# HGRN projections as seven of eight block products, head squares summed by ScalarE, and a VectorE copy of the last norm's factors

## The chip, the cores and the metric

The program runs on one core of a Trainium2 chip. The core has a matrix engine (TensorE, PE in the profile; its weight loads are listed as PEld), a vector engine (VectorE, DVE), a scalar engine (ScalarE, ACT), a general engine (GpSimd, POOL), and an engine that here only issues transfers (SyncE, SP). Each runs its own list of instructions in order and waits on semaphores for the others. The metric is the device time of one execution in microseconds (us); less is better.

## The reference

The reference is a trunk of two layers on one sequence of 1024 tokens with 1024 features, all in fp32. Each layer is a token mixer and a gated convolutional FFN, each behind an RMS norm whose scale, shift and gate come from a conditioning vector. Layer 0 mixes with a gMLP spatial gate, layer 1 with HGRN2, and a last RMS norm closes the trunk. The change lies in the HGRN2 mixer and in the last norm:

```python
def hgrn2_mixer(h, w_in, lb, gn_g, w_out):
    q, fz, i, g = jnp.split(h @ w_in, 4, axis=-1)
    f = lb + (1.0 - lb) * jax.nn.sigmoid(fz)
    k, q = 1.0 - f, jax.nn.silu(q)
    o = hgrn2_chunked_scan(heads(q), heads(k), heads(i), heads(jnp.log(f)))
    o = o * lax.rsqrt(jnp.mean(o * o, axis=-1, keepdims=True) + EPS)
    return (o.reshape(bsz, t, HG_HEADS * HG_VAL) * gn_g * jax.nn.silu(g)) @ w_out
...
x = x + g1 * y
...
return rms_norm(x, final_g)
```

There are 8 heads of 128 features. The scan gives `out[t] = q[t] . state[t]` with `state[t] = f[t] * state[t-1] + k[t] v[t]`, where v is i.

## The kernel before

**Number format.** Every large matrix product is done on pairs: an operand is split into a rounded part `hi` (made by ScalarE) and a rest `lo` (the source minus `hi`, made by VectorE or GpSimd), and `mm3` (line 272) issues three matmuls for each 128x128 block: hi·hi, hi·lo, lo·hi. `p_split` (lines 470 and 473) makes such a pair; its argument "V" or "G" says who subtracts.

**Order.** The kernel doesn't issue as it goes. Every step is entered in a list (`pl.op`) with its engine, an expected duration, what it reads and writes, and a place `pr`. A list scheduler runs over the steps once at the end with these durations, and the order it finds is the order of the instructions of each engine (and of the transfers, all of which SyncE issues). It treats GpSimd and those VectorE steps that are marked `port` as excluding each other.

**Stages.** In order: gMLP input products, spatial gate, output product; FFN of layer 0; HGRN2; its output product; FFN of layer 1; the last norm. Activations lie with features on partitions; the tokens form two halves, LO and HI, of 512 each. The residual `xT` (128 partitions x 8 feature blocks x 1024 tokens) stays in SBUF.

**Strassen-Winograd in the other stages.** The gMLP input products and the FFN (class `Pairs`) take two 128-row weight blocks at a time and cut weights and activations into 2x2 blocks: seven block products (`PRODUCTS`) in place of eight. Some products need sums of activation blocks (T1 to T4, built once by `combos`), others sums of weight blocks (built for each pair by `pair`: four VectorE sums, four pairs split by VectorE and three by GpSimd). `pair` also moves the products out of PSUM: `snap` copies by ScalarE, `add` adds by VectorE (line 701). The first pairs of a stage go the plain way with eight block products, while the sums are built. The output products (`block_out`, seven products named P1 to P7 in their order) use the same scheme.

**HGRN2 before.** Sixteen units, two for each head (LO and HI). For a unit, `project` computes f, q and g with `h_proj`, all eight block products: 3 x 24 matmuls of 512 columns. The values i come from `iproj` for two heads at a time with the tokens on partitions, as the scan needs them: 24 matmuls of 256 columns for each of 8 token blocks. `scan` then runs seven levels (line 1487 the matmuls, 1493 and 1497 the doubling steps of VectorE and ScalarE, 1470, 1519 and 1531 the score blocks), the state update (1549 to 1567), the outputs (1576, 1578), the head's norm (1580 squares by ScalarE, 1582 their sums by VectorE, a chain of ten small VectorE instructions, 1590 the scaling by VectorE), a transpose (1598) and the gain and gate (1600). Projections of the next unit stand between the scan's steps in PE's order. Units use banks 0 to 2 for projections, 3 and 4 for levels, 5 to 7 for the rest.

**Into the stage.** FFN 0 ends with the last block product; `f0_last` evacuates it into `xT` (412), sums squares, forms the norm's factors (333, the chain, 338, 343), and `ln_p` normalises each feature block: 448 by VectorE, then either hi by ScalarE (457) and lo by VectorE (458), or for every other block of HI two ScalarE steps and lo by GpSimd (462 to 464).

**The end.** `f1_last` works on the last 512 tokens in two parts of 256. Part 1's factors are copied from PSUM to SBUF by ScalarE (347), since GpSimd uses them from there; GpSimd multiplies five feature blocks by them (1692), VectorE the other three from PSUM, and then all of part 2.

## Time and profile before

| | |
|---|---|
| median of 3 runs | 2450.69 us (2450.42 to 2450.77) |
| the profiled execution | 2449.32 us, span 2447.5 us |
| PE, DVE, ACT, POOL busy | 2411.3, 1987.3, 1199.3, 473.3 us |
| HGRN2 stage (first projection to last head transpose) | 1194.67 to 1721.34 us |
| HBM read, written | 254.82 MB, 74.97 MB |

The span runs from the first instruction to the last; the rest of the profiled execution lies around it. "L272" is a line of the program, "pb" a PSUM bank, "n" the SBUF cells that hold the normalised activations in this stage, "w" and "h" cells for weights and intermediates, "wk" a work area. A group's busy time counts pipelined matmuls by their modelled ends, so that the start of one instruction to the start of the next is the better measure of what a matmul costs.

### The profile page before, as it was taken

The numbers are of one execution on the slowest core, as the hardware profiler recorded it, in microseconds if no ns is written. First come the engines' busy times: TensorE is split into PE (matmuls) and PEld (weight loads), VectorE is DVE, ScalarE is ACT, GpSimd is POOL, SyncE is SP. The second block draws the span as 40 slices with busy tenths as digits, with TensorE's granted clock in tenths as the row PEclk, the third lists the DMA queues.
The fourth block names the chain that finished last, engine by engine and source line by source line (L and its number), as shares of the span: only waits on it lengthen the run. The fifth ranks groups of instructions, "written<-read, shape, count | busy, mean of one in ns | idle before, by whom it ended". The sixth has DMA issues, their size and how long they took to land.

```text
span 2447.5 us, 33499 instructions
## 1 busy us (share of the span) xinstructions
PE 2411.3 (99%) x11870; PEld 2025.4 (83%) x11870; DVE 1987.3 (81%) x3176; ACT 1199.3 (49%) x2066; POOL 473.3 (19%) x289
## 2 busy tenths in 40 slices
PE   9999999999999999999999999999999999999998
PEld 7888788888788888888889898888777888888886
DVE  8888988898999888977846565657999989989756
ACT  5324665455555554445534444435455555554444
POOL 0222111222222221013211111100222222220121
PEclk9999999999999999999999999999999999999999
DMA  9897669720333324734111111123302332338333
GB/s 357 278 358 263 205 226 323 240 89 24 124 96 123 114 86 166 247 114 120 47 48 35 65 36 57 44 74 108 99 26 87 121 121 92 107 114 299 95 102 97
DMA packets 156266, 331.99 MB, mean 136 GB/s; under 512 B 15681, under 2 KB 34497, under 8 KB 156098
## 3 DMA queue, kind: packets, MB, share of 16 engines
q1 hardware_dynamic: 156098, 329.86, 40.5%
q8 instruction: 93, 1.52, 0.3%
q14 instruction: 75, 0.61, 0.1%
HBM read 254.82 MB, written 74.97 MB: 135 GB/s over the span
## 4 chain that ended last, share of the span: by engine, by line
PE 91%; DVE 4%; DMA 3%; ACT 1%; issue 1%; SPq 0%; DVEq 0%; ACTq 0%
PE pb L272 84%; PE pb L1487 3%; PE pb L1219 1%; DVE h L473 1%; PE pb L1556 1%; PE pb L1576 1%; PE pb L1578 0%; DMA xT<-vd 0%; DVE h L280 0%; PE pb L343 0%; DVE n L473 0%; DMA h<-in_ada 0%; DVE w L473 0%; PE pb L1549 0%; DMA w<-in_down 0%
## 5 line engine op out<-in xcount | busy, mean ns | idle before, releaser
L272 PE MATMUL pb<-h,w 128*128 128x512 f32 (+1 forms) x4212 | 977.6, 389 | 7.7 <-DVE h L473 2.5
L272 PE MATMUL pb<-n,w 128*128 128x512 f32 x3936 | 951.1, 393 | 8.0 <-DVE n L473 3.4
L272 PEld LDWEIGHTS pb<-h,w 128*128 128x128 f32 x4212 | 785.5, 188 | 175.2 <-DVE h L473 5.0
L272 PEld LDWEIGHTS pb<-n,w 128*128 128x128 f32 x3936 | 729.9, 188 | 160.8 <-DVE n L473 5.4
L473 POOL TENSOR_TENSOR w<-w,w 128x512 fp32r<-128x512 f32 x158 | 249.6, 1586 | 862.6 <-ACT w L470 761.4
L470 ACT ACTIVATE w<-w 128x512 fp32r<-128x512 f32 x384 | 237.1, 627 | 245.8 <-PE pb L272 144.4
L272 PE MATMUL pb<-w,n 128*128 128x512 f32 (+1 forms) x1536 | 272.5, 337 | 3.7 <-DVE n L458 3.4
L856 DVE SCALAR_TENSOR_TENSOR raw<-wk,prm,raw 128x1024 f32<-128x1024 f32 x168 | 267.4, 1602 | 5.4 <-ACT raw L852 4.2
L272 PEld LDWEIGHTS pb<-w,n 128*128 128x128 f32 x1536 | 238.3, 190 | 36.1 <-DVE n L458 3.9
L473 POOL TENSOR_TENSOR w<-raw,w 128x1024 fp32r<-128x1024 f32 (+1 forms) x48 | 115.2, 2409 | 529.0 <-ACT w L470 450.5
L473 DVE TENSOR_TENSOR w<-w,w 128x512 fp32r<-128x512 f32 x226 | 161.2, 718 | 40.1 <-ACT w L470 39.4
L470 ACT ACTIVATE w<-n 128x512 fp32r<-128x512 f32 x136 | 85.9, 632 | 173.3 <-PE pb L272 163.1
L698 ACT ACTIVATE wk<-pb 128x512 f32<-128x512 f32 x160 | 94.7, 593 | 136.6 <-PE pb L272 115.1
L473 DVE TENSOR_TENSOR w<-n,w 128x512 fp32r<-128x512 f32 x136 | 100.8, 744 | 60.1 <-ACT w L470 59.7
L701 DVE TENSOR_TENSOR wk<-pb,wk 128x512 f32<-128x512 f32 x160 | 108.4, 687 | 45.7 <-PE pb L272 41.2
L470 ACT ACTIVATE h<-h 128x512 fp32r<-128x512 f32 x198 | 122.1, 617 | 15.9 <-DVE h L473 5.8
L473 POOL TENSOR_TENSOR h<-h,h 128x512 fp32r<-128x512 f32 x48 | 67.9, 1416 | 256.0 <-ACT h L470 245.1
L852 ACT ACTIVATE raw<-wk,prm 128x1024 f32<-128x1024 f32 x84 | 103.6, 1240 | 26.0 <-DVE raw L480 11.5
L1493 DVE TENSOR_TENSOR wk<-wk 128x256 f32<-128x256 f32 x192 | 98.0, 534 | 21.8 <-PE pb L1487 11.1
L473 DVE TENSOR_TENSOR h<-h,h 128x512 fp32r<-128x512 f32 x150 | 109.4, 732 | 5.0 <-ACT h L470 5.0
L1497 ACT ACTIVATE wk<-wk 128x256 f32<-128x256 f32 x192 | 75.6, 417 | 77.1 <-PE pb L1487 61.9
L280 DVE SCALAR_TENSOR_TENSOR h<-h,raw 128x1024 f32<-128x1024 f32 x81 | 103.5, 1305 | 1.5 <-DMA h<-in_ada 1.5
(221 smaller groups left out, 2414.9 us busy)
## 6 DMA issues: line engine op xcount, KB each, us to landing
w<-in_up SPq DMA_DIRECT2D x88, 512.0 KB, 3.7
h<-in_ada SPq DMA_DIRECT2D x81, 512.0 KB, 5.8
act<-raw SPq DMA_DIRECT2D x154, 256.0 KB, 2.3
h<-act SPq DMA_DIRECT2D x124, 256.0 KB, 2.7
n<-in_down SPq DMA_DIRECT2D x64, 256.0 KB, 5.4
h<-gact SPq DMA_DIRECT2D x56, 256.0 KB, 4.0
gact<-xT SPq DMA_DIRECT2D x52, 256.0 KB, 3.7
vd<-h SPq DMA_DIRECT2D x32, 256.0 KB, 4.5
```

The source lines that it names most:

```text
L272: PE.matmul(ps, L[i // 2], R[i % 2], start=first and i == 0 and not more, stop=last and i == 2, skip_group_check=more)
L280: V.scalar_tensor_tensor(out=raw, in0=raw, scalar=1.0, in1=condr, op0=ALU.mult, op1=ALU.mult, accum_out=mod[:, m:m + 1])
L470: pl.op("S", 0.2 + 0.43 * w, lambda: S.activation(hi.r, src.f, AF.Copy), r=(src,), w=(hi,), pr=pr)
L473: lambda: e.tensor_tensor(out=lo.r, in0=src.f, in1=hi.f, op=ALU.subtract), *preds,
L698: pl.op("S", 0.6, lambda: S.activation(c.f, ps.f, AF.Copy), r=(ps,), w=(c,), pr=p(i) - 10)
L701: pl.op("V", 0.69, lambda: V.tensor_tensor(out=c.f, in0=ps.f, in1=c.f, op=ALU.add), r=(ps, c), w=(c,), pr=p(i) - 8)
L852: pl.op("S", 1.22, lambda: S.activation(y.f, wk[:, o + PADW:o + PADW + T], AF.Identity, bias=pc("conv_b", l * NUP + b), scale=cw(2)), r=(c ...
L856: pl.op("V", 1.26, lambda w=w: V.scalar_tensor_tensor(out=y.f, in0=wk[:, o + w:o + w + T], scalar=cw(w), in1=y.f, op0=ALU.mult, op1=ALU.ad ...
L1219: PE.matmul(ps.f[:, i * P:(i + 1) * P], v.f[:, i * P:(i + 1) * P], wsT[:, j, :], start=True, stop=True)
L1487: PE.matmul(ps_()[0:m, c, :], K.f[:, c * P:c * P + m], q, start=True, stop=True)
L1493: V.tensor_tensor(out=halves_(X2, s)[:, :, i, :], in0=halves_(X, s)[:, :, i, :], in1=pair2()[:, :, o].unsqueeze(2).to_broadcast([P, 256 // ...
L1497: S.activation(halves_(X2, s)[:, :, i, :], halves_(X, s)[:, :, i, :], AF.Copy)
```

## The change

1. The HGRN2 projections move to a new class `HgUp(Pairs)`: 16 pairs, for each head (f, q) and (i, g), both halves at once. The pairs of head 0 go the plain way (`plain`), the other 14 as seven block products. `combos` builds T1 to T4 from the normalised activations, which are now kept unshifted in `xT`.
2. For that, `xT` is stored to memory (`spill`, 16 transfers of 256 KB) once FFN 0 has written it, is then used as working space through the stage, and is loaded again (16 transfers) behind the units.
3. i now comes out with features on partitions like the others, and is transposed on PE (four 128x128 transposes for each unit) and copied back by ScalarE.
4. k = 1 - f moves from VectorE to ScalarE; the head's squares are summed by ScalarE's accumulation, four instructions of 128 columns; the scaling of the outputs also becomes four ScalarE instructions.
5. HI's normalised blocks are all finished by VectorE.
6. At the end, VectorE instead of ScalarE copies part 1's factors, after part 2's chain of small instructions, and all five GpSimd products wait for that.

```diff
+    xspill = dram.tile([P, KT, T], F32, name="xs")
...
+    def spill(hf, ds, pr):
+        for d in ds:
+            pl.op("D", 0.73, lambda d=d: nc.sync.dma_start(xspill[:, d, halves[hf]], xT[:, d, halves[hf]]),
+                  r=(xrg(d, halves[hf]),), w=(("xs", 2 * d + hf, 2 * d + hf + 1),), pr=pr)
...
+        spill(0, range(KT), pr)
+        ln_p(nms[0], 1, 0, rbv[0], lambda d: xv(d, LO), lambda d: pr + 20 + d)
...
-        ln_p(nms[1], 1, 0, rbv[1], lambda d: tring.next(), lambda d: at() + d, "VG")
+        ln_p(nms[1], 1, 0, rbv[1], lambda d: xv(d, HI), lambda d: at() + d)
...
+    class HgUp(Pairs):
+        def at(self, j, i):
+            return self.base + 10 * (j - 1) + 1 + i * 9 / 7
+        def bankof(self, j, i):
+            return (0, 1, 0, 1, 0, 1, 0)[i] if j == nu - 1 else (0, 1, 0, 2, 0, 2, 1)[i]
+        def weights(self, j):
+            return [a[("hgf", "hgq", "hgi", "hgg")[2 * (j % 2) + i]][j // 2] for i in range(2)]
+        def places(self, j):
+            return vgs(j // 2) if j % 2 else [*fqp[0], *fqp[1]]
+        def done(self, j, r, hf, pr):
+            x, h = self.places(j)[2 * r + hf], j // 2
+            if j % 2 == 0 and r == 0:
...
+            elif j % 2 and r == 0:
+                b = bv(mis.next())
+                def fn():
+                    for c in range(4):
+                        PE.transpose(b.f[:, cs(c)], x.f[:, cs(c)], ident)
+                pl.op("PE", 0.5, fn, r=(x,), w=(b,), pr=pr)
+                pl.op("S", 0.6, lambda: S.activation(x.f, b.f, AF.Copy), r=(b,), w=(x,), pr=pr)
+            elif j % 2:
...
+        def plain(self, j, prs):
...
...
-            op("V", 0.43, lambda: V.tensor_scalar(out=kk.f, in0=f.f, scalar1=-1.0, scalar2=1.0, op0=ALU.mult, op1=ALU.add),
-               (f,), (kk,), True)
+            op("S", 0.6, lambda: S.activation(k1.f, f.f, AF.Identity, scale=-1.0, bias=ones[:, 0:1]), (f,), (k1,))
...
-            op("S", 0.6, lambda: S.activation(sq.f, b3.f, AF.Square), (b3,), (sq,))
-            op("V", 0.7, lambda: V.tensor_reduce(out=small[:, 32:36], in_=sq.f.rearrange("p (c n) -> p c n", n=P),
-                                                 op=ALU.add, axis=mybir.AxisListType.X), (sq,), (sm,))
+            def squares():
+                for c in range(4):
+                    S.activation(sq.f[:, cs(c)], b3.f[:, cs(c)], AF.Square, accum_out=small[:, 32 + c:33 + c])
+            op("S", 1.3, squares, (b3,), (sq, sm))
...
-            op("V", 0.7, lambda: V.tensor_tensor(out=o.f.rearrange("p (c f) -> p c f", f=P),
-                                                 in0=b3.f.rearrange("p (c f) -> p c f", f=P),
-                                                 in1=r.unsqueeze(2).to_broadcast([P, 4, P]), op=ALU.mult),
+            def scaled():
+                for c in range(4):
+                    S.activation(o.f[:, cs(c)], b3.f[:, cs(c)], AF.Copy, scale=r[:, c:c + 1])
+            op("S", 1.3, scaled, (b3, ("small1", 0, 16)), (o,))
...
+    up.plain(0, (HB - 15, HB - 5))
+    for u in range(nu):
+        units[u].prepare(HB + 10 * u - 5)
+        if u == 0:
+            for k in TOP:
+                up.combos(k, HB + 1 + 0.5 * k, late=("T1", "T3"))
+            up.plain(1, (HB - 14, HB + 5))
...
+        if u and u % 2 == 0:
+            up.pair(u + 1)
+        prev = units[u].scan(HB + 10 * u, prev, *((lvs, mis) if u < nu - 2 else (Seq(2, 3),) * 2))
+        if u % 2 and u + 1 < nu:
+            up.pair(u + 1)
+    for hf, ds in ((0, TOP), (1, range(KT)), (0, range(4, KT))):
+        for d in ds:
+            p_load(pl, xv(d, halves[hf]), xspill[:, d, halves[hf]], HB + 10 * nu - 1, r=(("xs", 2 * d + hf, 2 * d + hf + 1),))
...
-        pl.op("S", 0.4, lambda: nms[1].copy_rb(bank[4][:, 0:256], rbv[1].f), b0, w=(rbv[1],), pr=at() - 4)
-        for d in (7, 0):
-            p_final(nms[1], d, 1, rbv[1], "G", at() - 3, b0)
...
-        for d in (1, 2, 3):
+        pl.op("V", 0.42, lambda: V.tensor_copy(rbv[1].f, bank[4][:, 0:256]), b0, c1, w=(rbv[1],), pr=at() - 2)
+        for d in (7, 0, 1, 2, 3):
             p_final(nms[1], d, 1, rbv[1], "G", at(), b0, c1)
```

More of the change, by code (lines that the diff above doesn't have):

```diff
@@ L635, in mid, with combos @@
             pass
-        def combos(self, k, pr, t1=None):
+        def combos(self, k, pr, t1=None, late=()):
             pl, w = self.pl, 3 * self.sub
@@ L653, in combos @@
             for i, (n, t) in enumerate((("T2", a22), ("T1", s1), ("T3", a12), ("T4", a21))):
-                if n != "T1" or t1 is None:
+                if n not in late and (n != "T1" or t1 is None):
                     p_split(pl, t, *self.b[n][k], "V", pr + 0.1 * i)
+        def at(self, j, i):
+            return self.base + 7 * j + i
+        def bankof(self, j, i):
+            return (4 * j + self.b0 + self.PRODUCTS[i][2]) % 8
         def product(self, j, i, slot, fine):
-            _, bn, bank_, more = self.PRODUCTS[i]
-            pl, pr = self.pl, self.base + 7 * j + i
-            ps = bv((4 * j + self.b0 + bank_) % 8)
+            _, bn, _, more = self.PRODUCTS[i]
+            pl, pr = self.pl, self.at(j, i)
+            ps = bv(self.bankof(j, i))
             hi, lo = slot
@@ L1318, in trunk, with xv @@
     nc_ = bc[10:11] + bc[2::3]
-    tring = Seq(*(v for c in nc_[0:2] for v in two(c, F32)))
+    xf = xT.rearrange("p k t -> p (k t)")
+    xl = Life("x", KT * T, ap=xf)
+    def xv(d, hs):
+        return View(xl, d * T + hs.start, HT)
+    def spill(hf, ds, pr):
+        for d in ds:
+            pl.op("D", 0.73, lambda d=d: nc.sync.dma_start(xspill[:, d, halves[hf]], xT[:, d, halves[hf]]),
+                  r=(xrg(d, halves[hf]),), w=(("xs", 2 * d + hf, 2 * d + hf + 1),), pr=pr)
     sqs2 = Seq(*two(nc_[2], F32))
@@ L1346, in trunk @@
     nu = 2 * NH
-    wsets = Seq(*((whole(x, F32R), whole(y, F32R)) for x, y in zip(f0.freed[0::2], f0.freed[1::2])))
-    wraw = Seq(rv(0), rv(1))
     kks, qqs, sts = (Seq(kv(o), kv(o + 512)) for o in (0, 1024, 2048))
@@ L1370, in trunk @@
-    t23 = rv(2, 0, 512), rv(2, 512, 512)
-    pjs, lvs, mis = Seq(0, 1, 2), Seq(3, 4), Seq(5, 6, 7)
+    fr = f0.freed
+    fqp = [parts(hc[i], 512, 512) for i in (10, 4)]
+    sigs = Seq(*parts(hc[0], 512, 512))
+    q1, k1 = parts(hc[6], 512, 512)
+    qx, = parts(hc[5], 768)
+    sc0, scs = rv(2, 512, 512), Seq(xv(6, HI), xv(7, HI))
+    ots = Seq(xv(4, LO), xv(5, LO))
+    gos = Seq(xv(6, LO), xv(7, LO), xv(2, HI), xv(3, HI))
+    hslots = [fr[9], fr[10], fr[11], hc[7], hc[9], hc[2], hc[8]]
@@ L1372, in trunk, with vgs @@
+    vg = [[xv(0, HI), xv(4, HI), xv(1, HI), xv(5, HI)], [xv(d, LO) for d in TOP]]
+    (v0, g0), vg7 = parts(hslots[6], 512, 512), [v for c in hslots[0:2] for v in parts(c, 512, 512)]
+    def vgs(h):
+        return [v0, vg[0][1], g0, vg[0][3]] if h == 0 else vg7 if h == NH - 1 else vg[h % 2]
+    lvs, mis = Seq(3, 4), Seq(5, 6, 7)
     lbc, omc = lbt[:, 3 * KT:4 * KT], lbt[:, 4 * KT:5 * KT]
     p_load(pl, masks, a["masks"], HB - 20)
-    hw, vtok, gout = {}, {}, {}
-    def h_weight(key, src, pr):
-        x = wraw.next()
-        hw[key] = hi, lo = wsets.next()
-        p_load(pl, x, src, pr)
-        p_split(pl, x, hi, lo, "G", pr)
+    gout = {}
@@ L1382, in sub @@
     def sub(v, o, n):
         return View(v.life, v.o + o, n)
-    def iproj(m, tb, pr):
-        hf = tb // 4
-        if tb % 4 == 0:
-            vtok[m, hf] = vts.next()
-        b, vt = bv(mis.next(), 0, 256), sub(vtok[m, hf], tb % 4 * 256, 256)
-        ts_ = slice(tb * P, tb * P + P)
-        for q in range(2):
-            ws = hw["i", m, q]
-            xs = [hop2(4 * q + k, ts_) for k in range(4)]
-            def fn(ws=ws, xs=xs, q=q):
-                hi, lo = (w.r.rearrange("p (k f) -> p k f", f=256) for w in ws)
-                for k, (xh, xl) in enumerate(xs):
-                    mm3(b.f, (xh.r, xl.r), (hi[:, k, :], lo[:, k, :]), q == 0 and k == 0, q == 1 and k == 3)
-            pl.op("PE", 1.45, fn, r=(*ws, *(v for x in xs for v in x)), w=(b,), pr=pr)
-        pl.op("S", 0.4, lambda: S.activation(vt.f, b.f, AF.Copy), r=(b,), w=(vt,), pr=pr)
@@ L1402, in h_proj @@
-    def h_proj(u, n, pr):
-        h, hs = u // 2, halves[u % 2]
-        hi, lo = hw[n, h]
-        b = bv(pjs.next())
-        for k0 in range(0, KT, 2):
-            xs = [hop2(k, hs) for k in (k0, k0 + 1)]
-            def fn(k0=k0, xs=xs):
-                for k, (xh, xl) in enumerate(xs, k0):
-                    c = slice(k * P, (k + 1) * P)
-                    mm3(b.f, (hi.r[:, c], lo.r[:, c]), (xh.r, xl.r), k == 0, k == KT - 1)
-            pl.op("PE", 1.362, fn, r=(hi, lo, *(v for x in xs for v in x)), w=(b,), pr=pr)
-        return b
@@ L1824, in _lay_out @@
     out["hgq"], out["hgf"], out["hgg"] = stat(hw[:, 0:D]), stat(hw[:, D:2 * D]), stat(hw[:, 3 * D:])
[L1825 removed]
+    out["hgi"] = stat(hw[:, 2 * D:3 * D])
     out["ho"] = f["hg_w_out"][0].reshape(NH, P, D)
```

137 lines of the change are left out of this document (63 added, 74 removed).

## The prediction

> **What bounds the kernel now.** The page first: which engine is busy, and which one the chain of work that ended last runs through.
>
> ```profile
> PE 2411.3 (99%) x11870; PEld 2025.4 (83%) x11870; DVE 1987.3 (81%) x3176; ACT 1199.3 (49%) x2066; POOL 473.3 (19%) x289
> PE 91%; DVE 4%; DMA 3%; ACT 1%; issue 1%; SPq 0%; DVEq 0%; ACTq 0%
> ```
>
> PE is the bound nearly throughout. The share of a whole run says little of one stage, so next comes the windows view of the HGRN2 stage alone (stretch and length, then busy us of PE, PEld, DVE, ACT and POOL with their instructions, granted clock, DMA share, GB/s), and PE's waits in it (total us, times, longest).
>
> ```profile
> 1194.67:1721.34 526.67, 525.75 (x3411) 468.31 (x3409) 333.71 (x833) 227.13 (x482) 79.20 (x37) 1.00 0.17 56
> PE pb L1549 <- DVE wk L1493: 0.7, 2, 0.4
> PE pb L272 <- DVE xT L412: 0.2, 1, 0.2
> ```
>
> In 526.7 us PE waits for 0.9. VectorE is busy 63% of it, ScalarE 43%, and the clock is at 1.00. So in this stage time goes down by what PE no longer has to issue, for as long as the other engines can follow. The groups of PE's instructions by shape, and a piece of its timeline (start, us, what), give what a projection matmul costs.
>
> ```profile
> L272 PE MATMUL pb<-n,w 128*128 128x512 f32 x1152 | 289.8, 399 | 0.0
> L272 PE MATMUL pb<-w,n 128*128 128x256 f32 x768 | 96.2, 284 | 0.0
> 1149.79 45.04 PE L272 MATMUL pb<-h,w 128*128 128x512 f32 x198
> 1194.67 6.96 PE L272 MATMUL pb<-n,w 128*128 128x512 f32 x30
> ...
> 1348.60 0.60 PE L1598 MATMUL pb<-prm,h 128*128 128x128 f32 x4
> 1348.95 1.64 PE L272 MATMUL pb<-n,w 128*128 128x512 f32 x6
> 1350.43 5.90 PE L272 MATMUL pb<-w,n 128*128 128x256 f32 x48
> 1356.17 1.00 PE L1487 MATMUL pb<-h,h 128*128 128x64 f32 x8
> ```
>
> Matmuls overlap, so their price is from start to start. 198 of 512 columns take 1194.67 - 1149.79 = 44.88 us: 0.2267 each. 48 of 256 columns take 5.74: 0.1196 each. Four transposes and six matmuls take 1350.43 - 1348.60 = 1.83; less 6 x 0.2267 that leaves 0.47 for a group of four transposes.
>
> **Part 1: PE.** Removed: 1152 x 0.2267 = 261.2 us (f, q, g) and 768 x 0.1196 = 91.9 us (i), together 353.1. Added: two plain pairs of 96 matmuls and 14 pairs of 7 x 12 = 84, all of 512 columns, 1368 x 0.2267 = 310.1; and 16 groups of transposes at 0.47, 7.5. Together 317.6. The scan's matmuls stay. **PE has 35.5 us less to issue.**
>
> **Part 2: VectorE must follow.** Its prices, from groups of this stage (and the add out of PSUM from the FFN's):
>
> ```profile
> L1434 DVE TENSOR_SCALAR h<-h 128x512 f32<-128x512 f32 x16 | 6.7, 421 | 13.3 <-ACT h L1432 13.3
> L1582 DVE TENSOR_REDUCE small<-h 128x4 f32<-128x512 f32 x16 | 10.9, 684 | 22.0 <-ACT h L1580 22.0
> L1590 DVE TENSOR_TENSOR h<-pb,small 128x512 f32<-128x512 f32 x16 | 10.9, 682 | 0.0
> L480 DVE TENSOR_TENSOR raw<-h 128x512 f32<-128x512 f32 x4 | 2.7, 683 | 0.0
> L473 DVE TENSOR_TENSOR n<-w,n 128x512 fp32r<-128x512 f32 x16 | 11.5, 727 | 1.2 <-PE pb L272 1.2
> L701 DVE TENSOR_TENSOR wk<-pb,wk 128x512 f32<-128x512 f32 x52 | 35.7, 689 | 20.5 <-PE pb L272 19.1 <-ACT wk L698 1.2
> ```
>
> Each unit loses k (0.42), the sums of squares (0.68) and the scaling (0.68): 16 x 1.79 = 28.6 us. Each of 14 pairs brings four weight sums (0.68), four splits (0.73) and four adds (0.69): 8.4, in all 117.6. `combos` brings four times four sums and four splits, 22.6, and HI's normalising four splits that GpSimd did, 2.9. VectorE goes from 333.7 to 448.2 us in a stage of 526.7 - 35.5 = 491.2: 91%. Does PE run freely beside such a VectorE? The FFN of layer 1 shows the same scheme, in its steady part and at its start:
>
> ```profile
> 2040.00:2120.00 80.00, 80.00 (x355) 66.27 (x354) 72.30 (x83) 41.54 (x61) 18.12 (x12) 1.00 0.31 109
> 1770.00:1850.00 80.00, 74.52 (x316) 58.74 (x314) 76.23 (x110) 44.77 (x70) 20.80 (x10) 0.98 0.08 27
> 1850.00:1880.00 30.00, 28.97 (x128) 23.65 (x127) 26.83 (x32) 15.71 (x24) 8.10 (x6) 1.00 0.38 129
> ```
>
> At 72.30 / 80 = 90% VectorE, with GpSimd at 23%, PE has no gap. At the start, where normalising, `combos` and the first pairs come together, VectorE is at 95% and PE loses 80 - 74.52 + 30 - 28.97 = 6.5 us.
>
> **Start of the new stage.** It has the same cover, two plain pairs, but two scans among it as well. From the factors on, at about 1206.7, VectorE has HI's normalising (16 steps of about 0.73, 12 us), `combos` (22.6), two units (333.7 / 16 - 1.8 = 19 each, an upper bound since the stage's other work is in it) and one pair (8.4): 81 us. PE has 144 of the 192 plain matmuls left (32.6), 19.0 of the first reduced pair, and two scans (what the 526.7 hold beside 353.1 of projections and about 22 of other products and sums: 151 / 16 = 9.4 each): 71 us. VectorE is about 10 us short at worst, and the row of the FFN, which is nearest, says 6.5. I take **+6.5**, with 0 and 24 (10 short and eleven GpSimd splits in the way) as ends.
>
> **Steady part.** Nothing (the FFN's 80.00 of 80) is one end, the rivals below the other. The scan is a chain of short steps and the FFN is not, so I take one short wait of about 0.2 us, such as the one in PE's list, for each of 14 pairs: **+3**.
>
> **ScalarE and GpSimd** have room. GpSimd's and ScalarE's rows:
>
> ```profile
> L473 POOL TENSOR_TENSOR w<-raw,w 128x1024 fp32r<-128x1024 f32 x28 | 68.2, 2441 | 370.1 <-ACT w L470 362.5 <-issue 7.6
> L473 POOL TENSOR_TENSOR w<-w,w 128x512 fp32r<-128x512 f32 x4 | 5.1, 1297 | 45.6 <-ACT w L470 45.6
> L470 ACT ACTIVATE n<-w 128x512 fp32r<-128x512 f32 x16 | 9.0, 622 | 5.1 <-PE pb L272 4.0 <-DMA w<-hact 1.0
> L1400 ACT ACTIVATE h<-pb 128x256 f32<-128x256 f32 x32 | 12.2, 382 | 41.5 <-PE pb L272 41.4
> L1580 ACT ACTIVATE h<-pb 128x512 f32<-128x512 f32 x16 | 9.6, 598 | 31.6 <-PE pb L1578 31.6
> ```
>
> ScalarE gains 106 weight splits at 0.62, 64 copies out of PSUM, 16 k and 16 transposed copies at 0.60, 16 splits of T, and for each unit eight instructions of 128 columns for one of 0.60. From 0.382 (256 columns) and 0.598 (512) such a quarter is about 0.28 (estimate). It loses some 32 wide splits and the 32 copies of L1400. The sum is near 341 of 491 us, 69%. No row shows the accumulating form: between nothing more and once more 0.28 for each of 64, at most 73%. Cost: 0, hidden by 30% of idle time. GpSimd's 28 wide splits become 42 of half the width (54 us), about 60 us in the stage for 79.
>
> **Transfers.** SyncE's queue gets 16 stores of 256 KB ahead of the stage and 16 loads behind the units, 4.2 MB each way. HI's in-place normalising must wait for its stores, but the sums and factors (1201 to 1207) lie between. The loads must be in before the output product's evacuations.
>
> ```profile
> 0.00:245.00 245.00, 239.68 (x1084) 199.13 (x1085) 209.35 (x373) 100.97 (x164) 44.57 (x26) 0.99 0.89 314
> 1698.51:1721.34 22.83, 22.67 (x147) 19.44 (x145) 19.85 (x49) 7.96 (x20) 0.70 (x1) 1.00 0.41 143
> ```
>
> At 314 GB/s 4.2 MB take 13 us, beside a stretch that already moves 143. The four blocks needed first are free since head 5, and the others are wanted one block product (48 x 0.2267 = 10.9 us) after another. I take 0; the other end is 13.
>
> **The last norm.** Timeline of the end:
>
> ```profile
> 2434.88 0.16 DVE L309 TENSOR_TENSOR small<-small 128x2 f32<-128x2 f32 x1
> ...
> 2435.07 0.67 DVE L310 TENSOR_TENSOR small<-small 128x2 f32<-128x2 f32 x1
> ...
> 2437.82 0.65 DVE L314 TENSOR_TENSOR small<-small 128x2 f32<-128x2 f32 x1
> 2438.50 0.16 DVE L315 TENSOR_TENSOR small<-small 128x2 f32<-128x2 f32 x1
> ...
> 2440.63 2.48 DVE L1692 TENSOR_TENSOR xT<-xT,pb 128x512 f32<-128x512 f32 x4 [0.98 <-PE pb L343]
> ...
> 2435.01 3.44 POOL L1692 TENSOR_TENSOR xT<-xT,h 128x256 f32<-128x256 f32 x5 [18.79 <-ACT h L347]
> ```
>
> While GpSimd's five products run (0.69 each), VectorE's small instructions take 0.65 in place of 0.16: five steps last 2438.50 - 2435.07 = 3.43 us where 5 x 0.2 would do. With GpSimd behind the chain 2.4 us go; VectorE's copy costs up to 0.4. Late next are GpSimd's products: begun near 2437.3 they end near 2440.8, and VectorE's last ones now near 2441.1. I take **-2.0**. The ends are -2.4 and +0.8, the latter if GpSimd stops VectorE's last four products at 0.69 each. The Trainium skill ("SBUF — State Buffer", Who interferes with whom) says that a VectorE instruction with two SBUF inputs excludes a GpSimd one that reads SBUF, and one with a single SBUF input does not; by that the five slow steps are explained, which the trace agrees with (0.65 beside 0.69), and the last four products, which read PSUM and SBUF, run freely, which no row here shows; the term stays -2.0.
>
> **Sum.** 2449.3 - 35.5 - 2.0 + 6.5 + 3 = **2421 us** in the terms of the profiled execution, which lies 1.4 under the median of the runs.
>
> **Rivals.**
>
> *VectorE and GpSimd exclude each other fully.* Then the stage needs 448 + 60 = 508 us of the two, or 521 with GpSimd's splits at 1.59 as in the page's longest group, against 491: 17 to 30 us over, and 2449.3 - 35.5 - 2.0 + 17 to 30 = 2431 to 2444 (the start's loss lies within).
>
> ```profile
> L473 POOL TENSOR_TENSOR w<-w,w 128x512 fp32r<-128x512 f32 x158 | 249.6, 1586 | 862.6 <-ACT w L470 761.4
> ```
>
> For it: the slow steps of the end. Against: in the FFN's steady part the two add up to 72.30 + 18.12 = 90.4 in 80 us without a gap on PE, since much of VectorE's work reads PSUM. The rule of the Trainium skill just named is this rival's mechanism. A start that loses 20 in place of 6.5 gives 2435, the same region. Chance 0.18.
>
> *Slower: the scan's waits stay on VectorE.* VectorE issues in order, and at the scan's steps it now waits for PE:
>
> ```profile
> DVE h L1470 <- PE pb L1487: 50.7, 32, 5.3
> ```
>
> It could afford that at 63%. What is queued behind such a wait is the next pair's sums, splits and adds, and PE's next block products wait for those. If all of these 50.7 us stay unfilled beside the 508, the stage lasts 559, and the time is 2449.3 - 35.5 - 2.0 + 68 = 2480. It is slower than before by over 0.2% from about 25 us of such idle time on (534 us of stage). For it: the order is fixed from expected durations. Against: the pairs' work is due a unit later and fits in these gaps, and PE's scan steps come earlier as fewer products stand between them. Chance 0.10.
>
> *xT comes back late.* PE waits at the output product for up to 10 us: 2431. Against it is the order of need above. Chance 0.06.
>
> **Chances.** The forecast, 2410 to 2430, has 0.66. The range is 2410 (no stall at all, and 2.4 at the end) to 2444 (full exclusion); it leaves out the slower rival and the upper edges. A measurement of this kernel can tell 0.2%, 4.9 us, from no change. Faster: 0.66 + 0.06 + nearly all of 0.18, 0.88. Within: 0.04, from the edges of the last two. Slower: 0.08.
>
> **What would show it.** In the trace after: 1368 matmuls of 512 columns in the stage and none of 256; the stage 491 to 505 us long; PE's waits in it near 10 us, most of them before the third pair, on VectorE's splits; VectorE near 90% with its waits at L1470's step mostly gone; the small chain of the end at 0.2 a step. If PE's waits are spread over all units, one of the first two rivals holds; if they lie at the first evacuations after the last unit, it is the loads. The forecast is wrong if VectorE's busy time rises far beyond 448 us.

## The result and the profile after

The median of the changed kernel is 2427.8 us (four runs, 2421.42 to 2429.21) beside 2450.73 us for the kernel before: a ratio of 0.9899, interval 0.9887 to 0.9911. The profiled execution took 2421.42 us (span 2419.6) beside 2449.32 (span 2447.5). The forecast of 2421 was made for a profiled execution, and this one is 27.9 us shorter. That it was hit to within 1 us is partly luck: the profiled execution is the fastest of the four, and between the medians lie 22.9 us.

The page after: the busy engines, and the chain that ended last.

```profile
PE 2381.8 (98%) x11382; PEld 1980.9 (82%) x11382; DVE 2070.5 (86%) x3334; ACT 1292.8 (53%) x2391; POOL 459.1 (19%) x303
PE 89%; DVE 6%; DMA 2%; issue 2%; ACT 1%; POOL 0%; SPq 0%; POOLq 0%; ACTq 0%; DVEq 0%
```

PE has 488 matmuls fewer and is still the bound. The windows view of the stage up to the last head transposes (columns as before: length, PE, PEld, DVE, ACT, POOL, clock, DMA share, GB/s):

```profile
1193.92:1693.90 499.98, 496.63 (x2943) 426.93 (x2942) 418.54 (x992) 322.98 (x807) 58.11 (x45) 1.00 0.21 65
1200.00:1300.00 100.00, 98.26 (x558) 83.56 (x557) 88.78 (x194) 67.79 (x152) 7.69 (x6) 1.00 0.08 24
```

499.98 us in place of 526.67, at full clock both times. In its first 100 us PE loses 1.7. PE's groups in the stretch from the first projection to the end of the output product's first part:

```profile
L273 PE MATMUL pb<-n,w 128*128 128x512 f32 x528 | 130.7, 398 | 1.4 <-ACT h L1468 1.4
L273 PE MATMUL pb<-n,h 128*128 128x512 f32 x336 | 84.4, 400 | 0.0
L273 PE MATMUL pb<-w,h 128*128 128x512 f32 x336 | 84.1, 399 | 0.0
L273 PE MATMUL pb<-n,n 128*128 128x512 f32 x133 | 35.6, 416 | 3.6 <-DVE n L474 2.3 <-ACT n L471 1.3
L273 PE MATMUL pb<-h,w 128*128 128x512 f32 x127 | 32.1, 396 | 0.0
...
L273 PE MATMUL pb<-w,w 128*128 128x512 f32 x42 | 11.8, 390 | 0.0
```

The projections are 528 + 336 + 336 + 127 + 42 = 1369 matmuls of 512 columns (1368, and one of the FFN's that runs into the window) and none of 256; the group n,n is the output product. What PE waits for in the stage and in the first part of the output product (total, times, longest):

```profile
PE pb L273 <- DVE n L474: 3.2, 2, 2.3
PE pb L1531 <- DVE h L1491: 1.9, 4, 0.5
PE pb L273 <- ACT h L1468: 1.4, 1, 1.4
PE pb L273 <- ACT n L471: 1.3, 1, 1.3
```

Two of the four lie behind the units, where the output product waits for its operands. PE's timeline there, of the changed kernel:

```profile
1687.98 5.70 PE L273 MATMUL pb<-n,n 128*128 128x512 f32 x24
1693.52 0.64 PE L1641 MATMUL pb<-prm,xT 128*128 128x128 f32 x4
1693.91 3.22 PE L273 MATMUL pb<-n,n 128*128 128x512 f32 x12
1698.42 0.73 PE L273 MATMUL pb<-n,n 128*128 128x512 f32 x2 [1.29 <-ACT n L471]
1701.47 4.38 PE L273 MATMUL pb<-n,n 128*128 128x512 f32 x11 [2.32 <-DVE n L474]
1706.77 5.52 PE L273 MATMUL pb<-n,n 128*128 128x512 f32 x23 [0.91 <-DVE n L474]
```

And of the kernel before, at the same place:

```profile
1720.98 0.60 PE L1598 MATMUL pb<-prm,h 128*128 128x128 f32 x4
1721.34 10.86 PE L272 MATMUL pb<-n,n 128*128 128x512 f32 x46
1734.33 5.96 PE L272 MATMUL pb<-n,n 128*128 128x512 f32 x25 [2.13 <-DVE n L473]
```

From the last head transposes to the last of these waits' end it is 1734.33 - 1720.98 = 13.35 us before and 1706.77 - 1693.52 = 13.25 after. The time is the same, but before PE had 46 matmuls for it and now 12 + 2 + 11 = 25. The others it had already done between the scan steps: the output product's first matmul starts 35.3 us ahead of these transposes (at 1658.20), and before it started 29.8 us ahead (at 1691.22).

Taken from the start of each PE instruction to the start of the next and added up by group, the stretch 1194.67 to 1734.33 (after: 1193.92 to 1706.77) divides so:

| us | before | after | difference |
|---|---|---|---|
| projections, with the transposes of i and PE's wait of 1.4 at the start | 367.1 | 331.2 | -35.9 |
| the scans | 137.0 | 141.6 | +4.5 |
| output product's part (n,n) | 34.2 | 38.8 | +4.6 |
| start of the stage | | | -0.8 |
| FFN of layer 1 | | | +1.1 |
| from the last 24 matmuls to the end | 17.84 | 16.38 | -1.5 |

The first three add up to -26.8, all six to the span's -27.9 but for rounding. (The last row is a stretch of its own, outside the first three.)

The end, in the timeline of the changed kernel:

```profile
2409.63 0.16 DVE L316 TENSOR_TENSOR small<-small 128x2 f32<-128x2 f32 x1
...
2410.36 0.42 DVE L1797 COPY h<-pb 128x256 f32<-128x256 f32 x1
...
2410.50 0.70 PE L344 MATMUL pb<-h,ones 128*128 128x256 f32 x2 [2.49 <-DVE h L339]
...
2410.86 3.45 POOL L1725 TENSOR_TENSOR xT<-xT,h 128x256 f32<-128x256 f32 x5 [21.09 <-DVE h L1797]
2411.31 2.48 DVE L1725 TENSOR_TENSOR xT<-xT,pb 128x512 f32<-128x512 f32 x4 [0.20 <-PE pb L344]
```

The small chain runs at 0.16 a step and the copy costs 0.42. GpSimd's five products end at 2414.31, VectorE's four at 2413.79: GpSimd is now the last.

### The profile page after: what moved, and what is told of

Its sections match the earlier page's. It is cut to its first block, busy times and chain, and to the rows that moved or that the text cites. A ratio compares the mean times of both kernels' runs of the same rounds, so it can differ in the third digit from the quotient of the medians.

```text
span 2419.6 us, 33107 instructions
## 1 busy us (share of the span) xinstructions
PE 2381.8 (98%) x11382; PEld 1980.9 (82%) x11382; DVE 2070.5 (86%) x3334; ACT 1292.8 (53%) x2391; POOL 459.1 (19%) x303
## 4 chain that ended last, share of the span: by engine, by line
PE 89%; DVE 6%; DMA 2%; issue 2%; ACT 1%; POOL 0%; SPq 0%; POOLq 0%; ACTq 0%; DVEq 0%
PE pb L273 81%; PE pb L1531 4%; PE pb L1227 1%; DVE h L474 1%; DVE w L474 1%; DVE n L474 1%; PE pb L1616 0%; DMA xT<-vd 0%; DVE raw L864 0%; PE pb L1596 0%; PE pb L1618 0%; DVE w L481 0%; DVE xT L481 0%; PE pb L344 0%; PE pb L1589 0%
## 5 line engine op out<-in xcount | busy, mean ns | idle before, releaser
L273 PE MATMUL pb<-h,w 128*128 128x512 f32 (+1 forms) x4338 | 1008.6, 388 | 6.1 <-DVE h L474 1.7
L273 PEld LDWEIGHTS pb<-h,w 128*128 128x128 f32 x4338 | 807.3, 188 | 178.5 <-DVE h L474 4.6
L273 PE MATMUL pb<-n,w 128*128 128x512 f32 x3312 | 791.9, 392 | 8.7 <-DVE n L474 2.9
L273 PEld LDWEIGHTS pb<-n,w 128*128 128x128 f32 x3312 | 616.7, 188 | 141.6 <-DVE n L474 4.9
L474 POOL TENSOR_TENSOR w<-w,w 128x512 fp32r<-128x512 f32 x158 | 252.2, 1602 | 854.7 <-ACT w L471 754.1
L471 ACT ACTIVATE w<-w 128x512 fp32r<-128x512 f32 x384 | 237.2, 627 | 233.5 <-PE pb L273 137.0
L474 DVE TENSOR_TENSOR w<-w,w 128x512 fp32r<-128x512 f32 x226 | 161.8, 721 | 39.3 <-ACT w L471 38.4
L273 PE MATMUL pb<-w,n 128*128 128x512 f32 x768 | 179.0, 395 | 3.6 <-DVE n L459 3.6
L273 PEld LDWEIGHTS pb<-w,n 128*128 128x128 f32 x768 | 146.0, 191 | 35.4 <-DVE n L459 4.1
L474 DVE TENSOR_TENSOR w<-n,w 128x512 fp32r<-128x512 f32 x136 | 99.4, 733 | 63.2 <-ACT w L471 62.6
L474 POOL TENSOR_TENSOR w<-raw,w 128x512 fp32r<-128x512 f32 (+1 forms) x52 | 83.9, 1622 | 334.6 <-ACT w L471 201.0
L860 ACT ACTIVATE raw<-wk,prm 128x1024 f32<-128x1024 f32 x84 | 103.6, 1240 | 33.0 <-DVE raw L481 13.2
L474 POOL TENSOR_TENSOR h<-h,h 128x512 fp32r<-128x512 f32 x48 | 70.4, 1466 | 252.4 <-ACT h L471 238.7
L474 DVE TENSOR_TENSOR h<-h,h 128x512 fp32r<-128x512 f32 x150 | 109.5, 732 | 4.9 <-ACT h L471 4.9
L413 DVE SCALAR_TENSOR_TENSOR xT<-pb,mod,xT 128x512 f32<-128x512 f32 (+1 forms) x120 | 83.0, 730 | 23.0 <-PE pb L273 22.2
L1537 DVE TENSOR_TENSOR wk<-wk 128x256 f32<-128x256 f32 x192 | 80.9, 445 | 10.6 <-PE pb L1531 6.9
```

What stands on the lines that cost most here:

```text
L273: PE.matmul(ps, L[i // 2], R[i % 2], start=first and i == 0 and not more, stop=last and i == 2, skip_group_check=more)
L413: V.scalar_tensor_tensor(out=xT[:, d, hs], in0=ps.f, scalar=gate(d), in1=xT[:, d, hs], op0=ALU.mult, op1=ALU.add)
L471: pl.op("S", 0.2 + 0.43 * w, lambda: S.activation(hi.r, src.f, AF.Copy), r=(src,), w=(hi,), pr=pr)
L474: lambda: e.tensor_tensor(out=lo.r, in0=src.f, in1=hi.f, op=ALU.subtract), *preds,
L860: pl.op("S", 1.22, lambda: S.activation(y.f, wk[:, o + PADW:o + PADW + T], AF.Identity, bias=pc("conv_b", l * NUP + b), scale=cw(2)), r=(c ...
L1537: V.tensor_tensor(out=halves_(X2, s)[:, :, i, :], in0=halves_(X, s)[:, :, i, :], in1=pair2()[:, :, o].unsqueeze(2).to_broadcast([P, 256 // ...
```

## The experiments

The theory: the time falls because PE has fewer matmuls to issue (P), and what is given back comes from places where PE has no work ready. The rivals: the stage is bound by VectorE, so that its work sets the time (V); GpSimd's splits stop VectorE and cost what they stop (E), against splits that run freely beside it (F); the transfers that bring xT back hold up the hand-over (Q), against the round trip through memory of the last head's own products (D), against the work on VectorE and ScalarE at the hand-over (W). And the runs of the changed kernel spread over 7.8 us, those of the kernel before, measured beside them, over 0.8: a wait of the new kernel that sometimes costs more, or the clock of a run (C, H).

**The changed kernel again**, with nothing edited, beside more runs of the kernel before.

> The changed kernel once more, with another profile. The four times of it so far run from 2421.4 to 2429.2 us, those of the kernel before from 2450.4 to 2451.2. Theory Q (the stored xT comes back through SyncE's in-order queue, and its timing decides how long PE waits at the output product): the spread comes back, 6 to 8 us, and a slower profile shows its extra time behind the last unit, at 1690 to 1710 us. Theory L (VectorE and GpSimd shut each other out in an order that differs from run to run): the extra time is spread over the HGRN2 stage, at the scan's first level. Theory C (the clock or the chip): the kernel before spreads as much in the same rounds.

2423.94 us (2423.0 to 2424.94), ratio 0.9884 (0.9871 to 0.9896). The kernel before took 2446.3 to 2456.39 in the 23 runs beside it. The spread belongs to both kernels: C holds.

**All pairs with eight block products**, the sums of activations and weights left out with them (the cut shows the main lines; the last pair's PSUM banks also change):

```diff
         if u == 0:
-            for k in TOP:
-                up.combos(k, HB + 1 + 0.5 * k, late=("T1", "T3"))
             up.plain(1, (HB - 14, HB + 5))
...
         if u and u % 2 == 0:
-            up.pair(u + 1)
+            up.plain(u + 1, (HB + 10 * u + 1, HB + 10 * u + 5))
...
         if u % 2 and u + 1 < nu:
-            up.pair(u + 1)
+            up.plain(u + 1, (HB + 10 * u + 1, HB + 10 * u + 5))
```

> The changed kernel with all 16 projection pairs as eight block products, without the sums T1 to T4 and the weight sums; the rest of the change stays (i transposed, head norm on ScalarE, xT stored and loaded). Theory P (the gain is PE's saved matmuls, less a few waits): PE issues 14 x 12 = 168 more matmuls at 0.2267 to 0.238, 38 to 40 us, and the 4 us or so of waits at the scan's steps go, so 2457 to 2463, somewhat slower than the kernel before. Rival (the gain comes from VectorE's relief or from another part of the change): within 10 us of the changed kernel.

2457.4 us (2455.51 to 2462.23), ratio 1.0024 (1.0015 to 1.0033): without the seventh product the rest of the change makes the kernel slower than before. The 14 pairs save 14 x 12 = 168 matmuls, by the price of the prediction 38.1 us; between this kernel and the changed one measured beside it lie 2457.4 - 2423.94 = 33.5. So 4.6 are given back, about what the scans take more: 141.6 us in the changed kernel, 136.8 in this one. P holds: PE's matmuls are what is saved.

Most of what makes it slower than the kernel before lies at the hand-over, where PE waits once for 7.2 us (2.1 before):

```profile
PE pb L273 <- ACT n L471: 7.2, 1, 7.2
```

Between the last head transposes and this wait PE has 33 matmuls. So the loss at the hand-over isn't a price of the seven products or of a shorter stage: it comes with the rest of the change, and with the order that the scheduler finds for it.

**The head's norm back on VectorE**: k, the sums of squares and the scaling as before the change.

```diff
...
-            def squares():
-                for c in range(4):
-                    S.activation(sq.f[:, cs(c)], b3.f[:, cs(c)], AF.Square, accum_out=small[:, 32 + c:33 + c])
-            op("S", 1.3, squares, (b3,), (sq, sm))
+            op("S", 0.6, lambda: S.activation(sq.f, b3.f, AF.Square), (b3,), (sq,))
+            op("V", 0.7, lambda: V.tensor_reduce(out=small[:, 32:36], in_=sq.f.rearrange("p (c n) -> p c n", n=P),
+                                                 op=ALU.add, axis=mybir.AxisListType.X), (sq,), (sm,))
...
```

> The changed kernel with k, the sums of squares and the scaling of the head norm back on VectorE (28.6 us of VectorE in the stage, from 418 to about 447 of 500, 89%; ScalarE about 36 us less). Theory P (VectorE has room in the steady part; only the hand-over to the output product is bound by it): PE's waits at the scan's first level stay near 2 us, the hand-over waits grow by up to 1.8 us, the time by 0 to 3 us. Theory V (the moves to ScalarE are what makes the seven products pay): about 1.8 us for each of 14 units, 25 us, so 2448.

2426.84 us (2424.3 to 2434.59), ratio 0.9902 (0.9885 to 0.9919). Its stage, in the windows view, and PE's waits:

```profile
1194.00:1694.00 500.00, 493.07 (x2909) 424.12 (x2908) 427.25 (x1025) 281.57 (x608) 58.69 (x44) 0.99 0.20 64
```

```profile
PE pb L273 <- DVE n L474: 3.9, 4, 1.8
PE pb L273 <- ACT h L1468: 1.9, 1, 1.9
...
```

VectorE does 28.6 us more by the prediction's prices, and its busy time in this window rises by 8.7 only; over the whole run it rises by 15.9 (2070.5 to 2086.4 on the pages), and the rest stays open. The changed kernel stood at 0.9899, 0.9884 and 0.9900 in its three series of runs: the difference is at most 0.0018, some 4 us, with intervals that overlap, and a bound on VectorE would make it some 25. V falls. Here the scheduler leaves 44 matmuls behind the last head transposes, and PE waits 2.7 us there: a stage just as short, with a better cover. The three edits of the head's norm together are worth a few us at most.

**GpSimd's splits given to VectorE**, in the projections alone:

```diff
-        plainfunc, b0 = AF.Copy, 0
+        plainfunc, b0, ge = AF.Copy, 0, "G"
...
-            p_split(pl, a11, *slots[0], "G", p(-6))
-            p_split(pl, a12, *slots[1], "G", p(-5))
+            p_split(pl, a11, *slots[0], self.ge, p(-6))
+            p_split(pl, a12, *slots[1], self.ge, p(-5))
...
-            p_split(pl, a22, *slots[6], "G", p(0))
+            p_split(pl, a22, *slots[6], self.ge, p(0))
...
     class HgUp(Pairs):
+        ge = "V"
```

> The changed kernel with the three GpSimd splits of each of the 14 reduced pairs done by VectorE: 42 x 0.73 = 30.7 us more for VectorE, none for GpSimd in the steady part. Theory E (the two exclude each other for whole instructions, so a GpSimd split costs VectorE what it would cost to do it): VectorE's busy time rises by less than 31 us because its waits for GpSimd go, and the time stays within 3 us. Theory F (GpSimd's splits run beside VectorE's work out of PSUM nearly for nothing): VectorE rises by the full 31 us to 90% of the stage, PE's waits in the stage grow from 5 to 15 us or more, and the time by 8 us or more.

2421.0 us (2420.04 to 2423.06), ratio 0.9872 (0.9858 to 0.9885). VectorE got 41 splits more, 28 us of work. Its stage:

```profile
1194.00:1694.00 500.00, 498.45 (x2959) 429.56 (x2958) 422.54 (x1037) 323.97 (x811) 6.48 (x5) 1.00 0.21 67
```

VectorE's busy time is 422.5 in place of 418.5. Where the other 24 us went is seen in part in its groups by shape, of the changed kernel first:

```profile
L1537 DVE TENSOR_TENSOR wk<-wk 128x256 f32<-128x256 f32 x192 | 80.9, 445 | 10.6 <-PE pb L1531 6.9 <-ACT xT L706 1.7 <-PE pb L1618 1.3
...
L1537 DVE TENSOR_TENSOR wk<-h,h 128x256 f32<-128x256 f32 x32 | 16.8, 525 | 2.3 <-PE pb L1531 2.1
...
L1493 DVE TENSOR_TENSOR h<-h,h 128x512 f32<-128x512 f32 x16 | 14.8, 923 | 0.3
```

and of this experiment:

```profile
L1537 DVE TENSOR_TENSOR wk<-wk 128x256 f32<-128x256 f32 x192 | 76.4, 421 | 9.9 <-PE pb L1531 4.7 <-ACT xT L706 1.8 <-ACT h L706 1.6
...
L1537 DVE TENSOR_TENSOR wk<-h,h 128x256 f32<-128x256 f32 x32 | 13.4, 420 | 1.5 <-PE pb L1531 1.4
...
L1493 DVE TENSOR_TENSOR h<-h,h 128x512 f32<-128x512 f32 x16 | 11.6, 724 | 0.3
```

These are steps with two SBUF inputs, and each kind is shorter without GpSimd beside it (0.923 to 0.724, 0.525 to 0.420); these three groups make up 11 us. With 28 us more work, the durations of all VectorE steps in the stretch add up to 475.3 in place of 467.0: about 20 us were waiting for GpSimd. The scan's four waits at L1531 are gone from PE's list, and the scans take 137.9 us where they took 141.6 in the changed kernel and 137.0 before (added up as in the table). E holds and F falls: GpSimd's splits account for 3.7 of the 4.5 us that the scans had become dearer. The price was no higher, presumably because VectorE has 16% left.

**The same kernel a second time**, beside the changed kernel a third time, to set that price.

> The kernel of split_v again, beside the changed kernel on the same chip: 2 to 4 us less than it (its stage was 3.7 us shorter in the trace, its scan waits gone).

> The changed kernel again, as the measure for the other three on this chip: 27 to 29 us less than the kernel before, with a spread of some us in both. Theory H (the spread is the clock, which is granted at half for a few us after PE has waited, at the start, at the hand-over and at the second FFN's start): the lowered clock in this profile lies in these places again and its sum goes with the time.

2419.71 us (2418.84 to 2420.02, ratio 0.9876, 0.9862 to 0.9891) beside 2424.13 (2422.66 to 2430.64, ratio 0.9900, 0.9883 to 0.9917): 4.4 us between the medians. No run of the one reaches the other, though the intervals of the ratios overlap. Of H, the places hold in the changed kernel's trace (granted clock 0.50 or 0.51 from 9.2 to 19.4, 1702.2 to 1705.6 and 1821.7 to 1825.1 us); whether the sum goes with the time is taken up at the end.

**xT not loaded again.** This kernel leaves out the 16 loads of xT behind the units, so the residual that follows is what the stage left there.

```diff
-    for hf, ds in ((0, TOP), (1, range(KT)), (0, range(4, KT))):
-        for d in ds:
-            p_load(pl, xv(d, halves[hf]), xspill[:, d, halves[hf]], HB + 10 * nu - 1, r=(("xs", 2 * d + hf, 2 * d + hf + 1),))
```

> The changed kernel without the 16 loads that bring xT back; the residual that the output product adds to is then whatever the stage left there. Theory Q: PE's waits behind the last unit (4.5 us in the trace after) fall to the 2.3 of the kernel before or less, so 2 to 5 us less than the changed kernel, and the spread of its runs shrinks to 1 to 2 us. Theory L: PE's waits there stay at 4 us, since VectorE's splits run beside GpSimd's; no change and the same spread.

2424.67 us (2420.67 to 2424.96), ratio 0.9883 (0.9870 to 0.9896), as the changed kernel beside it (2423.94). PE's waits in the stage:

```profile
PE pb L273 <- ACT n L471: 3.0, 1, 3.0
...
PE pb L273 <- DVE n L474: 1.2, 1, 1.2
```

The hand-over still waits 3.0 + 1.2. The loads cost nothing that the time or these waits show; Q falls.

**GpSimd's four sums at the hand-over given to VectorE.**

```diff
-                p_sum(pl, nms[0], d, accv[0], sqs, pr, "VG"[d < 4])
+                p_sum(pl, nms[0], d, accv[0], sqs, pr, "VG"[d < 4 and l == 0])
```

> The changed kernel with the four sums of squares that GpSimd does while the output product begins (1.3 to 1.9 us each, beside them VectorE's splits take 1.7 in place of 0.7) given to VectorE. Theory E (the hand-over is VectorE's, and GpSimd's lock makes it longer): PE's waits between the last unit and the third block product fall from 4.5 to 2 or less, and the clock dip behind them goes, so 2 to 4 us less. Rival (it is VectorE's amount of work alone): 4 x 0.7 = 2.8 us more for VectorE there, waits of 5 to 7 us.

2425.03 us (2422.15 to 2428.68), ratio 0.9886 (0.9868 to 0.9904). The hand-over waits 2.7 + 1.3 in place of 4.5: nothing that the time can show. Neither the 2 or less of E nor the 5 to 7 of its rival came.

**No GpSimd at the hand-over**: the splits of the projections, these sums, the splits of the output product and of FFN 1's first pair all on VectorE (the two edits above, and these).

```diff
-            p_split(pl, x, *at[i, m], "VG"[i > 2 and m % 2], pr)
+            p_split(pl, x, *at[i, m], "VG"[i > 2 and m % 2 and not narrow], pr)
...
-                    p_split(pl, View(x.life, 512 * c, 512), *w[r, c], "G", p(-6 + c))
+                    p_split(pl, View(x.life, 512 * c, 512), *w[r, c], "V" if self.l and not j else "G", p(-6 + c))
```

> split_v, and in the hand-over to the output product and the first FFN pair behind it VectorE also does GpSimd's four sums of squares and its splits. Theory E (a GpSimd instruction there holds up VectorE's next two-input step, 1.75 in place of 0.68, about 1.07 us for each of five, and costs 0.68 when VectorE does it): PE's waits at the hand-over fall from 4.4 in split_v to 2 to 3 us, and the time by 1 to 3 us against split_v, part of it because the clock no longer dips. Rival (VectorE's amount of work): waits of 5 us or more.

2416.98 us (2409.02 to 2419.69), ratio 0.9855 (0.9833 to 0.9877), 2.7 under the kernel with the projections' splits alone (2419.71) beside it, with ranges that overlap. One wait is left at the hand-over, in PE's timeline:

```profile
1690.74 0.60 PE L1641 MATMUL pb<-prm,xT 128*128 128x128 f32 x4
1691.10 7.77 PE L273 MATMUL pb<-n,n 128*128 128x512 f32 x33
1701.91 28.44 PE L273 MATMUL pb<-n,n 128*128 128x512 f32 x111 [3.04 <-ACT n L471]
```

E said 2 to 3 us of waits and 1 to 3 us less time, and both came, the time not clear of the spread: the waits are 3.0 in place of 4.3 in the second trace of the projections' splits, and the last of them ends 11.2 us after the head transposes (1701.91 - 1690.74) in place of 13.2. So the slowed steps held a part of the hand-over. With VectorE free of GpSimd 3.0 us of wait remain, and something else holds those.

**The last head's sum read where it lies.** P6 needs, of the last pair of heads, a sum that VectorE has just made in SBUF; the kernel stores it to memory and loads it again. Here, on top of the last kernel, it is split from SBUF; the load falls away, the store stays.

```diff
-            x = braw.next()
-            part, rg = act(m, b)
-            p_load(pl, x, part, pr - 1.5, r=(rg,))
+            x = direct.get((m, b))
+            if x is None:
+                x = braw.next()
+                part, rg = act(m, b)
+                p_load(pl, x, part, pr - 1.5, r=(rg,))
...
-              ho_first, ho_last, tail=2, narrow=True, early=20, sets0=(s0_, t0_), ahead=8, b0=4)
+              ho_first, ho_last, tail=2, narrow=True, early=20, sets0=(s0_, t0_), ahead=8, b0=4,
+              direct={(NH // 2 - 1, 4): rv(2, 512, 512)})
```

> no_gps, and the last activation block that the third block product waits for (head 7's sum, made by the last unit) is split from where it lies in SBUF, without being stored to memory and loaded again. Theory D (the hand-over is bound by the round trip through memory of the last unit's output, about 5 us): PE's waits there go to 1 us or none, 3 to 5 us less than no_gps. Theory W (it is bound by VectorE's queue, which is busy without a break from 1682 to 1706 us): 0 to 1.5 us less.

2411.48 us (2409.31 to 2414.26), ratio 0.9844 (0.9829 to 0.9859). PE's timeline behind the last head transposes:

```profile
1686.33 0.60 PE L1643 MATMUL pb<-prm,xT 128*128 128x128 f32 x4
1686.68 40.53 PE L273 MATMUL pb<-n,n 128*128 128x512 f32 x177
```

177 matmuls run through. D holds: what remained of the wait was the round trip through memory. Against W stands that VectorE and ScalarE still do the sum, the split and everything else here. The 34th matmul behind the transposes starts 7.9 us after them (0.35 + 33 x 0.229), with the round trip 11.17 us after: 3.3 us. Behind its wait the kernel with the round trip also runs at a granted clock of 0.50 from 1701.2 to 1708.0, and its 111 matmuls take 0.256 each where these take 0.229: 3.0 us more. Together that is 6.3 us at the hand-over. The medians are 5.5 apart, with ranges that overlap (2409.02 to 2419.69 without this edit). The two profiles are 8.0 apart, but 4.3 of that lie ahead of the HGRN2 stage (it begins at 1197.34 without the edit and at 1193.03 with it), ahead of everything that was edited. This version has the lowest median, 12.7 us under the changed kernel beside it, and no run of it reaches one of either kernel of this study.

**The last norm alone**, put on the kernel before:

```diff
-         pl.op("S", 0.4, lambda: nms[1].copy_rb(bank[4][:, 0:256], rbv[1].f), b0, w=(rbv[1],), pr=at() - 4)
-         for d in (7, 0):
-             p_final(nms[1], d, 1, rbv[1], "G", at() - 3, b0)
...
-         for d in (1, 2, 3):
+         pl.op("V", 0.42, lambda: V.tensor_copy(rbv[1].f, bank[4][:, 0:256]), b0, c1, w=(rbv[1],), pr=at() - 2)
+         for d in (7, 0, 1, 2, 3):
```

> Only the edit of the last norm, on the kernel before. Theory T1 (the prediction's term): 2.0 us less, small VectorE steps at 0.2 us each. Theory T2 (from the trace after: the chain loses 2.9 us but the last store now waits for GpSimd's five products, which end after VectorE's): 1.4 us less, the last GpSimd product ending after the last VectorE one. Both: nothing else moves; ratio about 0.9993.

2451.32 us (2446.42 to 2454.7), ratio 0.9993 (0.9984 to 1.0003): by its time inconclusive. In the trace the stretch from the last 24 matmuls to the end is 16.96 us, against 17.84 before and 16.38 in the changed kernel. Its broadcast and products:

```profile
2442.11 1.22 PE L343 MATMUL pb<-h,ones 128*128 128x256 f32 x2 [2.49 <-DVE h L338]
...
2442.47 3.46 POOL L1692 TENSOR_TENSOR xT<-xT,h 128x256 f32<-128x256 f32 x5 [21.08 <-DVE h L1764]
2443.44 2.48 DVE L1692 TENSOR_TENSOR xT<-xT,pb 128x512 f32<-128x512 f32 x4 [0.72 <-PE pb L343]
```

The same broadcast took 1.22 here and 0.70 in the changed kernel, which is most of the 0.6 between the two. It took 1.22 in the kernel before as well, and the granted clock beside it was 0.50 in both and 1.00 in the changed kernel. So 17.84 and 16.96 compare like with like: the edit is worth 0.9, and the rest of the changed kernel's 1.5 is its clock.

The scheduler orders the whole program anew for each of these kernels, so some hundred instructions of PE stand elsewhere in each of them; differences of one or two us between two kernels can come from that.

## Why the prediction was right, step by step

- **PE's matmuls (-35.5): right as a difference**, -35.9 with the 1.4 of the start's wait within it, -37.3 without. The two sides were each too low: 367.1 us went in place of 353.1, and 329.8 came in place of 317.6. The price of 0.2267 is that of one long run of matmuls; in the stage, where groups of twelve stand between scan steps, a projection matmul takes 0.2367 (329.8 less 5.9 for the transposes, over 1368). The two errors cancel, all but 1.8 us. The kernel with all pairs plain shows that it is these matmuls.
- **Start of the stage (+6.5): too large.** It cost 1.4, one wait on ScalarE (L1468, the copy of a plain product out of PSUM), not on VectorE's splits. The step that failed is that VectorE would be 10 us short there: from 1200 to 1300 VectorE is busy 88.78 us of 100, full but not behind.
- **Steady part (+3): the size was off.** The scans take 4.5 more, and 168 matmuls saved 33.5 in place of 38.1. Only 1.9 of it are waits that the profile lists, for VectorE's step L1491, but 3.7 of it go when GpSimd's splits go to VectorE: it is the mechanism of the first rival, at a small part of its price.
- **Where PE's waits would lie: wrong.** Most were to lie before the third pair. They lie at the hand-over.
- **Hand-over (0, with 13 as the end): the step that was left out.** The prediction priced xT's loads there, rightly at nothing, and said that waits at this place would mean them. It did not ask how much PE work stands between the last head's steps and the first product that needs them. That cover went from 46 matmuls to 25, and the 13 us of the hand-over showed: +4.6, of which 2.2 are waits (4.5 in place of 2.3) and about 1.7 a lower clock behind them (granted 0.50 from 1701.7 to 1705.1). Of the 13 us, GpSimd beside VectorE's last steps is worth about 2 and the round trip through memory at least 3.3. What sets the cover is the scheduler's order and not the saved work: it is 33 with all pairs plain (7.2 us of waits) and 44 with the head's norm on VectorE (2.7).
- **The last norm (-2.0): too large.** -1.5 in the changed kernel's trace, -0.9 by itself at a like clock. The chain went from slow steps to 0.16, as said, but GpSimd's products became the last, 0.5 us behind VectorE's in the changed kernel and level with them in the kernel with this edit alone.
- **VectorE's busy time (448): 418.5 measured.** The durations, added up by group, come to 467, above the forecast by about the 20 us of waiting for GpSimd; but the busy time counts overlapping steps once, and steps of 0.68 follow each other every 0.60 (those of L481 and L474 in the changed kernel start at 1703.03, 1703.63 and 1704.23). The forecast added durations to a busy time.
- **Rivals.** Full exclusion of VectorE and GpSimd exists as a mechanism (the split experiment) and was hidden by idle time, all but 3.7 us. Its price was added up wrongly: 2449.3 - 35.5 - 2.0 + 17 to 30 is 2429 to 2442, so its lower end lies inside the forecast's 2410 to 2430. The range's own low end, 2449.3 - 35.5 - 2.4, is 2411. The scan's waits, the slower rival, went away as argued against it: the step that waited 50.7 us for PE (L1470, now L1514) shows 8.1, and 0.9 more where it writes another cell.

VectorE's waits in the stage, of the changed kernel:

```profile
DVE xT L1514 <- PE pb L1531: 8.1, 12, 1.7
```

That the sum came out at the forecast is luck as far as these terms go: the start was too dear by 5.1 us and PE's saving too small by 1.8, the hand-over too cheap by 4.6, the scans by 1.5 and the last norm by 0.5. What was right is the main term, that PE's matmuls set the time of this stage.

## What to carry to other kernels

When the order of a stage changes, count what PE still has to do behind its last step, because filler work that used to hide a fixed delay may now stand ahead of it, whether the stage got shorter or not; then shorten the delay, here by keeping GpSimd away from VectorE's last steps and by reading the last operand where it lies. A full VectorE beside GpSimd is judged by its steps with two SBUF inputs: their mean duration with and without GpSimd gives the price, and moving GpSimd's work over can be cheaper than sharing. Durations of one engine's steps and its busy time are two measures, and one isn't added to the other.
